# In-place pair differences, earlier residual sums and six landing pages in the second block of a two-block kernel

## The chip, the cores and the metric

One core of a Trainium2 chip runs the whole program. The metric is the device time of one execution in microseconds, the median of several runs. TensorE (PE) does the matrix products, VectorE (DVE), ScalarE (ACT) and GpSimd (POOL) the elementwise work, SyncE (SP) issues nearly all transfers. Each engine works through its own queue in order.

## The reference, cut to what matters

A first block (a gated spatial mixer, then windowed attention) yields x, 1024 tokens by 1024 features. The change lies in the second block:

```
hl = modulate(rmsnorm(x, norm1_g), sh1, sc1)
gate_b, gate_c, hv = split(hl @ conv_w_in, 3)          # 1024 x 3072
yl = (gate_b * conv3_grid(gate_c * hv, conv_w)) @ conv_w_out
x = x + g1 * yl
h = modulate(rmsnorm(x, norm2_g), sh2, sc2)
gate, up = split(h @ ffn_w_in, 2)                      # 2 x 2816 columns
x = x + g2 * ((silu(gate) * up) @ ffn_w_out)
return rmsnorm(x, final_g)
```

All in fp32. The kernel makes an fp32 product from three fp32r products of 512 columns: each operand is split into a high part (a cast on ACT, L106) and a remainder (a subtraction on DVE, L107); high by high, high by remainder and remainder by high are added in PSUM.

## The kernel before, in words

**Seven products.** Every large product of the second block is done in halves of tokens, features and columns with seven half-size products instead of eight (Winograd's form). P1 to P7 need the quarters of the right operand (B11, B21, B12) and four combinations of them (T1 = B22 - B21, T3 = B12 - B22, T2 = B12 - T1, T4 = B11 - T2), and four combinations S1 to S4 of the left one.

**Stages of the second block.** (1) `right_operands` (L1172) forms T1 to T4 of the normalised x per block of 128 tokens and splits them into seven slots (`H`, `HB`), four slices t to a slot. (2) `run_sets` (L1277) runs the sets of 128 output columns of `conv_w_in`, seven products of 12 matmuls each; a set's `use` does the gate and the convolution. After two or three sets a pair of results is complete, and `spill` (L1363) stores B11, B21, B12, forms T1 to T4 on POOL and stores them to DRAM. Beside that `sums` (L1419) forms S1 to S4 of the next weight (`conv_w_out`, `ffn_w_out`): load two blocks into two units, add on POOL, store, load the next, in six steps for each pair; `mix.tick()` takes some of those steps at each set's end. (3) `out_products` (L1428) multiplies by `conv_w_out`: for each of P1, P2, P6, P7, P5, P4, P3 in this order it loads right operand and weight (or weight sum) in pairs of 128 rows, splits them into pages and runs 6 matmuls for each of four token blocks and each index of a pair; P1, P6, P5, P3 add up in PSUM banks 0 to 3, P2, P7, P4 in 4 to 7. Its results go through `out_use` (L1631) and `conv_use` (L1645): gate, residual X2 from DRAM, then `third` (L1610): norm, transposes, modulate, split into slots N3. (4) The same for the feed-forward: four columns in eight-product form (`eight`, its "early" half needs only B11 and B21 of all tokens), 18 sets, `out_products` with `ffn_use` and `fourth` (final norm, output).

**Buffers.** `E` holds 18 units `U(i)` of 128x512. In the sets they are handed out by `Units`, first in first out: `get` takes the oldest free one, so its wait is for whatever still reads it. `RAW` is a ring of landing buffers of 128x1024 (`next_raw`): four in the conv stages, three in the last one. Weights that aren't sums land there, and so do those that `eight` loads. Right operands and sums in `out_products` land in `inner`, a ring of four (conv) or eight (feed-forward). Split pages in `out_products` are a ring too: 8 in the conv stage, 14 in the last.

**Order of the work.** The program order is written by hand, but a planner (with its own estimate of durations) puts each engine's queue in order; it may bring work forward past program order where data and buffers allow. What it can't do is take a ring's buffer before the earlier user in program order has let it go. A transfer, too, holds a buffer until it is done: a store's source can be rewritten only after the store has completed.

Of the kernel before, what the change touches and what calls it, by code (L numbers as in the profile page):

```python
# [10 lines left out]
ALU = mybir.AluOpType  # L11
# [16 lines left out]
def program(tc, I, out):  # L28
# [4 lines left out]
    with ctx:  # L33
# [771 lines left out]
        xs2 = ring([ZX[:, 0:1024]])  # L805
        hs2 = ring([ZX[:, 1024:1536]])
# [7 lines left out]
        junk = sb(P2, "junk", 512)  # L814
# [357 lines left out]
        def right_operands(where, t, h1, h2, eng):  # L1172

            b11, b21, b12, b22 = h1[:, 0:512], h1[:, 512:1024], h2[:, 0:512], h2[:, 512:1024]
            split_slots(("B12",), where, t, b12)
            V.tensor_tensor(b21, b22, b21, ALU.subtract)
            eng.tensor_tensor(b22, b12, b22, ALU.subtract)
            V.tensor_tensor(b12, b12, b21, ALU.subtract)
            eng.tensor_tensor(b11, b11, b12, ALU.subtract)
            split_slots(("T2", "T3"), where, t, h2)  # L1180
            split_slots(("T4", "T1"), where, t, h1)
# [95 lines left out]
        def run_sets(sets, where, units):  # L1277
# [12 lines left out]
            for n, (st, use) in enumerate(sets):  # L1290
# [72 lines left out]
        def spill(dst, j, even, odd, units):  # L1363

            (b11, b12), (b21, b22) = even, odd
            ids = [units.get() for _ in range(4)]
            t1, t2, t3, t4 = (U(i) for i in ids)
            if b11 is None:
                ids += [units.get() for _ in range(2)]
                b11, b21 = (U(i) for i in ids[4:])  # L1370
                SY.dma_start(b11, dst["B11"][j])
                SY.dma_start(b21, dst["B21"][j])
            else:
                SY.dma_start(dst["B11"][j], b11)
                SY.dma_start(dst["B21"][j], b21)
            SY.dma_start(dst["B12"][j], b12)
            G.tensor_tensor(t1, b22, b21, ALU.subtract)
            SY.dma_start(dst["T1"][j], t1)
            G.tensor_tensor(t2, b12, t1, ALU.subtract)
            SY.dma_start(dst["T2"][j], t2)  # L1380
            G.tensor_tensor(t3, b12, b22, ALU.subtract)
            SY.dma_start(dst["T3"][j], t3)
            G.tensor_tensor(t4, b11, t2, ALU.subtract)
            SY.dma_start(dst["T4"][j], t4)
            units.put(*ids)

        def sums_steps(w, j, dst, a, b):

            def block(m, k):
                return w[(2 * j + k - 1) * 128:(2 * j + k) * 128, (m - 1) * 512:m * 512]  # L1390

            def s0():
                SY.dma_start(a, block(2, 2))
                SY.dma_start(b, block(2, 1))

            def s1():
                G.tensor_tensor(a, a, b, ALU.add)
                SY.dma_start(dst["S1"][j], a)
                SY.dma_start(b, block(1, 2))

            def s2():
                G.tensor_tensor(b, a, b, ALU.subtract)
                SY.dma_start(dst["S2"][j], b)
                SY.dma_start(a, block(1, 1))

            def s4():
                G.tensor_tensor(a, a, b, ALU.subtract)
                SY.dma_start(dst["S4"][j], a)
                SY.dma_start(b, block(2, 2))

            def s5():
                SY.dma_start(a, block(1, 2))

            def s3():
                G.tensor_tensor(a, a, b, ALU.subtract)
                SY.dma_start(dst["S3"][j], a)
            return [s0, s1, s2, s4, s5, s3]

        def sums(w, nj, dst, bufs):  # L1419

            steps = []
            for j in range(0, nj, 2):
                two = [sums_steps(w, i, dst, U(bufs[2 * (i - j)]), U(bufs[2 * (i - j) + 1])) for i in range(j, min(j + 2, nj))]
                for x in zip(*two) if len(two) == 2 else [(y,) for y in two[0]]:
                    steps.extend(x)
            return steps
# [109 lines left out]
        for t in range(4):  # L1536
# [7 lines left out]
            right_operands(N1, t, a, b, G if t < 3 else V)  # L1544
# [5 lines left out]
        units = Units(14, 15, 8, 9, 10, 11, 12, 13)  # L1550
        spill(TC, 0, (None, U(16)), (None, U(17)), units)
        units.put(16, 17)
# [20 lines left out]
        def gate(j):  # L1573
            def use(c11, c12, c21, c22, free):
# [4 lines left out]
                spill(TC, j, *((cv[:, 0:512], cv[:, 512:1024]) for cv in cvs), units)  # L1579
                cvs.clear()  # L1580
                if j == 1:
                    mix.begin(sums(c_out, 4, SC, [units.get() for _ in range(4)]), 5)
# [13 lines left out]
        xsr = ring([U(12, 2), U(14, 2)])  # L1596
# [13 lines left out]
        def third(i, xs, junk):  # L1610

            t = i % 4
            SY.dma_start(X3[i], xs)
            for h in range(2):
                mean_square(MS[:, i, h:h + 1], xs[:, h * 512:(h + 1) * 512], junk)
            rms(RM[:, i:i + 1], MS[:, i, :])
            xn, hs = next_raw(), next_raw()
            V.tensor_scalar(xn, xs, RM[:, i:i + 1], None, op0=ALU.mult)
            for h in range(2):
                feature_blocks(xn[:, h * 512:(h + 1) * 512], hs[:, h * 512:(h + 1) * 512], h,  # L1620
# [5 lines left out]
            else:  # L1626
                h1 = next_raw()
                SY.dma_start(h1, HR3[t])
                right_operands(N3, t, h1, hs, G if t < 3 else V)

        def out_use(name, t, ps):  # L1631

            u2, u3, r = U(t), U(4 + t), U(8 + t)
            if name in ("P1", "P6"):
                A.copy(u2, ps)
            elif name == "P2":
                V.tensor_tensor(r, ps, u2, ALU.add)
                G.tensor_tensor(r, r, gbs[0], ALU.mult)
            elif name == "P5":
                A.copy(u3, ps)  # L1640
                V.tensor_tensor(u3, PS[:, 4 + t], u3, ALU.add)
                G.tensor_tensor(u3, u3, gbs[1], ALU.mult)  # L1642
            return u2, u3, r

        def conv_use(name, t, ps):  # L1645
            u2, u3, r = out_use(name, t, ps)
            if name == "P5" and t < 2:
                halves[t]["load"]()
            elif name == "P4":
                xs = xsr()  # L1650
                SY.dma_start(xs, X2[t])
                G.tensor_tensor(xs[:, 0:512], xs[:, 0:512], r, ALU.add)
                V.tensor_tensor(r, ps, u2, ALU.add)
                V.tensor_tensor(r, r, gbs[1], ALU.mult)
                V.tensor_tensor(xs[:, 512:1024], xs[:, 512:1024], r, ALU.add)
                third(t, xs, r)
            elif name == "P3":
                if t == 0:
                    halves[0]["early"](N3, (6, 7), early_up(0))
                xs = xsr()  # L1660
                SY.dma_start(xs, X2[4 + t])
                G.tensor_tensor(xs[:, 512:1024], xs[:, 512:1024], u3, ALU.add)
                V.tensor_tensor(u2, ps, gbs[0], ALU.mult)
                V.tensor_tensor(xs[:, 0:512], xs[:, 0:512], u2, ALU.add)
                third(4 + t, xs, u2)
                if t < 3:
                    f = t + 1
                    if f > 1:
                        halves[f]["load"]()
                    halves[f]["early"](N3, ((0, 6), (1, 7), (2, 0))[t], early_up(f))  # L1670
# [21 lines left out]
        for f in range(4):  # L1692
            halves[f]["late"](N3, ((4, 5), (6, 7))[f % 2], late_up)
            units.put(*halves[f]["keep"])
            if f % 2:
                spill(TF, f // 2, (None, U(ys[0])), (None, U(ys[1])), units)
                units.put(*ys)
                ys.clear()

        def gated_up(f):  # L1700
            def use(c11, c12, c21, c22, free):
# [9 lines left out]
                if f % 2:  # L1711
                    spill(TF, f // 2, *((U(a), U(b)) for a, b in ys), units)
                    units.put(*ys[0], *ys[1])
                    ys.clear()
                if f == 7:
                    mix.begin(sums(f_out, NFF // 2, SF, [units.get() for _ in range(4)]), NFF - 9)
# [13 lines left out]
        xsr = ring([U(12, 2), U(14, 2)])  # L1730

        def fourth(i, halves):
            rms(RX[:, i:i + 1], MS[:, i, :])
            for h in (1, 0):
                c = slice(h * 512, (h + 1) * 512)
                V.scalar_tensor_tensor(halves[h], halves[h], RX[:, i:i + 1], FG[:, c], ALU.mult, ALU.mult)  # L1736
                SQ("l").dma_start(out[0, i * 128:(i + 1) * 128, c], halves[h])

        def ffn_use(name, t, ps):
            u2, u3, r = out_use(name, t, ps)  # L1740
            if name == "P5":
                x = next_raw()[:, 0:512]
                SY.dma_start(x, X3[4 + t][:, 512:1024])
                G.tensor_tensor(u3, u3, x, ALU.add)  # L1744
                mean_square(MS[:, 4 + t, 1:2], u3, x)
            elif name == "P4":
                xs = xsr()
                SY.dma_start(xs, X3[t])
                G.tensor_tensor(xs[:, 0:512], xs[:, 0:512], r, ALU.add)
                V.tensor_tensor(r, ps, u2, ALU.add)  # L1750
                V.tensor_tensor(r, r, gbs[1], ALU.mult)  # L1751
# [60 lines left out]
```

## Time and profile before

| | before |
|---|---|
| median of 3 runs | 2709.69 us (2708.47 to 2711.11) |
| profiled execution, its own time | 2709.77 us |
| its span, first to last instruction | 2708.0 us |
| PE busy | 2588.4 us, 96% |
| DVE busy | 1841.7 us, 68% |
| ACT busy | 1102.5 us, 41% |
| POOL busy | 656.7 us, 24% |
| DMA, mean | 156 GB/s |

The second block starts at about 1623 us of the span. Its sets of the convolution run to about 1890, the product with `conv_w_out` to 1979, the feed-forward's start to 2120, its sets to 2476, the last product to the end. PE is busy nearly all the time, so what a stage loses shows as PE idle or as a lower granted clock after it; a busy share of the whole span doesn't show it, a table of stretches does.

### The profile page before, as it was taken

The page shows a single profiled execution, that of the slowest core. Times are in us where ns is not written, and L with a number is a line of the kernel's source. Part 1 is how long each engine was busy: PE and PEld are TensorE (multiplying, and loading weights), DVE is VectorE, ACT ScalarE, POOL GpSimd, SP SyncE. Part 2 cuts the span into 40 slices and gives each one's busy share as a digit, 9 for nine tenths or more (in the row PEclk, how much of TensorE's full clock was granted, in tenths as well). Part 3 has the DMA queues.
Part 4 walks back from the last instruction along what each step waited for, and adds up shares of the span by engine and source line. Part 5 has one row for each costly group of instructions (what it writes and reads, how often), then busy time and mean ns, then how long its engine had stood idle before and what let it go on. Part 6 is the DMA issues. An engine that isn't in the chain of part 4 may idle for free. (4 is left out here: it accounts for less than half of the span.)

```text
span 2708.0 us, 37147 instructions
## 1 busy us (share of the span) xinstructions
PE 2588.4 (96%) x13666; PEld 2216.0 (82%) x13666; DVE 1841.7 (68%) x3013; ACT 1102.5 (41%) x1979; POOL 656.7 (24%) x634
## 2 busy tenths in 40 slices
PE   8999999999999999999999987999878999999998
PEld 5799998879999778888888876877756877787876
DVE  5677775666778875456677977678566765667536
ACT  4332334322233435345556875223454232334433
POOL 2110000010002412313345762041321345302111
PEclk9999999999999999999999998999989999999999
DMA  7454333364444435541364325356554478538643
GB/s 258 141 148 122 101 119 125 121 205 135 130 137 133 146 103 189 174 155 61 92 244 133 98 78 167 109 183 194 179 181 149 151 253 260 181 103 287 195 151 129
DMA packets 344938, 421.18 MB, mean 156 GB/s; under 512 B 18918, under 2 KB 207870, under 8 KB 344242
## 3 DMA queue, kind: packets, MB, share of 16 engines
q1 hardware_dynamic: 337012, 407.80, 47.0%
q10 hardware_dynamic: 7744, 11.01, 1.1%
q8 instruction: 107, 1.75, 0.3%
q14 instruction: 75, 0.61, 0.1%
HBM read 324.84 MB, written 93.91 MB: 155 GB/s over the span
## 5 line engine op out<-in xcount | busy, mean ns | idle before, releaser
L106 ACT CAST w<-raw 128x1024 fp32r<-128x1024 f32 (+1 forms) x234 | 221.7, 958 | 437.5 <-DMA raw<-in_a_w_in 121.9
L107 DVE TENSOR_TENSOR w<-raw,w 128x1024 fp32r<-128x1024 f32 (+1 forms) x232 | 288.1, 1253 | 152.7 <-ACT w L106 148.3
L1265 PE MATMUL PS<-H,w 128*128 128x512 f32 x1404 | 336.8, 395 | 14.1 <-ACT E L1302 10.7
L1265 PEld LDWEIGHTS PS<-H,w 128*128 128x128 f32 x1404 | 267.2, 191 | 74.5 <-ACT E L1302 12.3
L516 PE MATMUL PS<-H,w 128*128 128x320 f32 x2112 | 320.5, 309 | 1.0 <-DVE TT L525 1.0
L516 PEld LDWEIGHTS PS<-H,w 128*128 128x128 f32 x2112 | 310.8, 188 | 3.1 <-DVE TT L525 1.3
L1456 PE MATMUL PS<-H 128*128 128x512 f32 x924 | 220.4, 397 | 12.3 <-ACT H L106 10.5
L1456 PEld LDWEIGHTS PS<-H 128*128 128x128 f32 x924 | 176.7, 192 | 52.3 <-ACT H L106 12.2
L339 POOL TENSOR_TENSOR H<-ACC,H 128x256 fp32r<-128x256 f32 x52 | 50.3, 968 | 609.6 <-ACT H L338 505.1
L320 DVE SCALAR_TENSOR_TENSOR ACC<-raw,CO,ACC 128x512 f32<-128x512 f32 x182 | 133.8, 747 | 20.6 <-DMA raw<-in_ada_w 17.9
L516 PE MATMUL PS<-H 128*128 128x320 f32 x960 | 144.7, 309 | 0.0
L516 PEld LDWEIGHTS PS<-H 128*128 128x128 f32 x960 | 141.1, 188 | 0.5
L603 PE MATMUL PS<-w,H 128*128 128x512 f32 x600 | 140.1, 391 | 0.0
L1265 PE MATMUL PS<-HB,w 128*128 128x512 f32 x540 | 135.7, 400 | 2.9 <-ACT E L1302 2.5
L603 PEld LDWEIGHTS PS<-w,H 128*128 128x128 f32 x600 | 111.5, 188 | 23.3
L107 DVE TENSOR_TENSOR PTR<-PS,PTR 128x512 fp32r<-128x512 f32 x176 | 106.1, 613 | 35.9 <-ACT PTR L106 34.4
L1265 PEld LDWEIGHTS PS<-HB,w 128*128 128x128 f32 x540 | 102.3, 190 | 28.2 <-ACT E L1302 3.4
L1339 PE MATMUL PS<-H,w 128*128 128x512 f32 x408 | 106.2, 413 | 19.3 <-ACT E L1347 9.1
L392 PE MATMUL PS<-H 128*128 128x512 f32 x510 | 120.9, 391 | 0.0
L870 ACT ACTIVATE s<-s,sm 128x641 f32<-128x641 f32 (+1 forms) x128 | 103.3, 808 | 42.6 <-DVE sm L868 42.0
L107 DVE TENSOR_TENSOR H<-raw,H 128x1024 fp32r<-128x1024 f32 x68 | 88.6, 1306 | 46.6 <-ACT H L106 45.2
L106 ACT CAST H<-raw 128x1024 fp32r<-128x1024 f32 x68 | 70.6, 1043 | 110.1 <-DMA raw<-in_a_w_in 63.2
(356 smaller groups left out, 5201.8 us busy)
## 6 DMA issues: line engine op xcount, KB each, us to landing
raw<-in_a_w_in SPq DMA_DIRECT2D x96, 512.0 KB
raw<-in_ada_w SPq DMA_DIRECT2D x80, 512.0 KB
raw<-in_ffn_w_in SPq DMA_DIRECT2D x76, 256.0 KB
E<-in_ffn_w_out SPq DMA_DIRECT2D x66, 256.0 KB
raw<-in_a_w_out SPq DMA_DIRECT2D x32, 512.0 KB
TFT<-E SPq DMA_DIRECT2D x44, 256.0 KB
SFS<-E SPq DMA_DIRECT2D x44, 256.0 KB
raw<-in_b_w_in SPq DMA_DIRECT2D x20, 512.0 KB
```

The costliest lines, as they stand in the source:

```text
L106: A.copy(hi, src)
L107: turn["split"] = (eng or V).tensor_tensor(lo, src, hif, ALU.subtract)
L320: V.scalar_tensor_tensor(ACC[:, s, :], r[:, j, :], CO[:, c, k:k + 1], ACC[:, s, :], ALU.mult, ALU.add)
L339: G.tensor_tensor(AL.r[:, 256:512], ACC[:, s, c], AL.f[:, 0:256], ALU.subtract)
L392: T.matmul(ps, HT[0][:, k, ap, t * 128:(t + 1) * 128], w[:, k % 2, :], start=k == 0 and n == 0, stop=k == 7 and n == 2)
L516: T.matmul(pss[h][:, 0:320], w[:, k, :], HT[0][:, k, ap, h * 320:(h + 1) * 320], start=k == 0 and n == 0, stop=k == 7 and n == 2)
L603: turn["mm"] = T.matmul(accs[t], ys[j].r[:, ap * 640 + t * 128:ap * 640 + (t + 1) * 128], wv[:, j, :], start=kp == 0 and j == 0 and n == 0 ...
L870: A.activation(out=p[:, :nk + 1], in_=p[:, :nk + 1], func=AF.Exp, scale=-1.0, bias=sm[:, j:j + 1], accum_out=sm[:, 2 + j:3 + j])
L1265: turn["mm"] = T.matmul(ps, w[:, k, :], b[:, ap, k, :], start=start and k == 0 and n == 0, stop=k == 3 and n == 2, skip_group_check=not start)
L1339: turn["mm"] = T.matmul(ps, x[:, k, :], b[:, ap, k, :], start=start and k == 0 and n == 0, stop=stop and k == 3 and n == 2, skip_group_che ...
L1456: turn["mm"] = T.matmul(ps[:, t], x[ap][:, i, t * 128:(t + 1) * 128], s[v][:, i, :], start=new and j + i == 0 and q == 0, stop=j + i == nj ...
```

## The change

- `right_operands`: all four subtractions on DVE (before: two of the four on POOL for t < 3).
- `spill`: T1 to T4 overwrite B21, B22, B12, B11 in place, in the order T1, T3, T2, T4; no units are taken for them. `late_spill` does so for pairs whose B11 and B21 come back from DRAM.
- `sums`: a step now does both indices of a pair of pairs, and `run_sets` has a second `mix.tick()` in the middle of each set; the number of ticks over which the steps are spread goes from 5 to 12 and from 13 to 26.
- `out_use` takes over the residual for both stages: halves of X are loaded where P2, P7, P5 and P4 end, added and squared there, so that P4 and P3 add one half each. P2 and P5 take a landing buffer of `RAW` for each of four token blocks. Every token block has its own units; the ring `xsr` of two goes.
- `third` and `fourth` take the two halves; X3 is stored and normalised in halves.
- `out_products` for `conv_w_out`: 6 landing pages and 7 split pages instead of 4 and 8.
- The small buffer `junk` of the attention is allocated earlier in its pool.

```
-        def right_operands(where, t, h1, h2, eng):
+        def right_operands(where, t, h1, h2):
...
-            eng.tensor_tensor(b22, b12, b22, ALU.subtract)
+            V.tensor_tensor(b22, b12, b22, ALU.subtract)
...
                     head(nxt)
+                mix.tick()
...
+        def spill(dst, j, even, odd):
+            (b11, b12), (b21, b22) = even, odd
+            for name, x in (("B11", b11), ("B21", b21), ("B12", b12)):
+                SY.dma_start(dst[name][j], x)
+            pair_sums(dst, j, b11, b12, b21, b22)
+
+        def pair_sums(dst, j, b11, b12, b21, b22):
+            for name, o, x, y in (("T1", b21, b22, b21), ("T3", b22, b12, b22), ("T2", b12, b12, b21),
+                                  ("T4", b11, b11, b12)):
+                G.tensor_tensor(o, x, y, ALU.subtract)
+                SY.dma_start(dst[name][j], o)
...
+        def out_use(X, name, t, ps, done):
+            u2, u3, r, x = U(t), U(4 + t), U(8 + t), U(12 + t)
+
+            def gated_add(u, gb, i, h):
+                G.tensor_tensor(u, u, gb, ALU.mult)
+                y = next_raw()[:, 0:512]
+                SY.dma_start(y, X[i][:, h * 512:(h + 1) * 512])
+                G.tensor_tensor(u, u, y, ALU.add)
+                mean_square(MS[:, i, h:h + 1], u, y)
+
+            if name in ("P1", "P6"):
+                A.copy(u2, ps)
+            elif name == "P2":
+                V.tensor_tensor(r, ps, u2, ALU.add)
+                gated_add(r, gbs[0], t, 0)
+            elif name == "P7":
+                SY.dma_start(x, X[t][:, 512:1024])
+            elif name == "P5":
+                A.copy(u3, ps)
+                V.tensor_tensor(u3, PS[:, 4 + t], u3, ALU.add)
+                gated_add(u3, gbs[1], 4 + t, 1)
+            elif name == "P4":
+                V.tensor_tensor(u2, ps, u2, ALU.add)
+                V.tensor_tensor(u2, u2, gbs[1], ALU.mult)
+                V.tensor_tensor(u2, u2, x, ALU.add)
+                SY.dma_start(x, X[4 + t][:, 0:512])
+                mean_square(MS[:, t, 1:2], u2, PS[:, 4 + t])
+                done(t, r, u2)
+            else:
+                tmp = next_raw()[:, 0:512]
+                V.tensor_tensor(tmp, ps, gbs[0], ALU.mult)
+                V.tensor_tensor(x, x, tmp, ALU.add)
+                mean_square(MS[:, 4 + t, 0:1], x, tmp)
+                done(4 + t, x, u3)
...
         def conv_use(name, t, ps):
+            if name == "P3" and t == 0:
+                halves[0]["early"](N3, (6, 7), early_up(0))
+            out_use(X2, name, t, ps, third)
             if name == "P5" and t < 2:
                 halves[t]["load"]()
...
-        out_products(c_out, 4, TC, SC, pages[2:], [p.f[:, q * 1024:(q + 1) * 1024] for p in pages[:2] for q in range(2)],
+        out_products(c_out, 4, TC, SC, pages[3:], [p.f[:, q * 1024:(q + 1) * 1024] for p in pages[:3] for q in range(2)],
```

## Rows read from the trace of the kernel before

**Rows 1.** The profiled page: its span, and the group of weight-splitting subtractions.
```profile
span 2708.0 us, 37147 instructions
...
L107 DVE TENSOR_TENSOR w<-raw,w 128x1024 fp32r<-128x1024 f32 (+1 forms) x232 | 288.1, 1253 | 152.7 <-ACT w L106 148.3
```
**Rows 2.** Stretches: length, busy us (count) of PE, PEld, DVE, ACT, POOL, PEclk, DMA, GB/s.
```profile
1620.00:1680.00 60.00, 46.39 (x186) 36.96 (x185) 44.06 (x72) 31.77 (x58) 16.74 (x11) 0.87 0.57 180
...
1880.00:1940.00 60.00, 50.90 (x206) 40.25 (x205) 36.98 (x34) 24.92 (x29) 17.31 (x10) 0.91 0.73 232
1956.00:2000.00 44.00, 29.86 (x134) 23.00 (x132) 31.76 (x63) 21.67 (x51) 14.83 (x13) 0.82 0.46 162
2000.00:2080.00 80.00, 71.70 (x301) 54.90 (x302) 49.69 (x75) 40.33 (x71) 13.85 (x10) 0.97 0.44 141
...
2200.00:2320.00 120.00, 108.85 (x442) 86.67 (x441) 73.47 (x83) 32.19 (x52) 62.39 (x43) 0.94 0.78 256
2320.00:2460.00 140.00, 140.00 (x611) 114.35 (x610) 95.05 (x115) 47.98 (x74) 28.21 (x19) 1.00 0.42 137
...
2620.00:2640.00 20.00, 14.68 (x52) 10.97 (x51) 7.48 (x8) 8.46 (x16) 11.94 (x8) 0.83 0.56 167
2694.00:2708.00 14.00, 0.62 (x3) 0.19 (x1) 9.21 (x20) 2.00 (x6) 2.61 (x4) 0.63 0.55 206
```
**Rows 3.** Waits of PE from 1600 us on: us in total, times, longest.
```profile
PE PS L1265 <- ACT E L1302: 13.2, 6, 4.9
...
PE PS L1339 <- ACT w L106: 7.7, 4, 4.5
```
**Rows 4.** Timeline in the feed-forward's sets, 2196 to 2222 us: start, duration, instruction, idle before.
```profile
2209.92 0.38 SPq L1384 DMA_DIRECT2D TFT<-E  x1
...
2214.56 0.63 ACT L1706 ACTIVATE E<-E 128x512 f32<-128x512 f32 x1 [13.69 <-DMA TFT<-E]
...
2215.72 6.45 PE L1265 MATMUL PS<-H,w 128*128 128x512 f32 x20 [2.41 <-ACT E L1302]
```
**Rows 5.** Waits of SP's queue, 2140 to 2460 us.
```profile
SPq L1382 <- POOL E L1381: 30.9, 6, 10.6
```
**Rows 6.** Timeline at the second block's start.
```profile
1658.51 0.68 DVE L1178 TENSOR_TENSOR E<-E 128x512 f32<-128x512 f32 x1
...
1659.27 4.05 POOL L1179 TENSOR_TENSOR E<-E 128x512 f32<-128x512 f32 x1 [4.21 <-DVE E L1178]
...
1663.35 1.14 ACT L1167 CAST HB<-E 128x512 fp32r<-128x512 f32 x2 [2.69 <-POOL E L1179]
...
1666.44 10.49 PE L1339 MATMUL PS<-H,w 128*128 128x512 f32 x38 [4.50 <-ACT w L106]
```
**Rows 7.** Timeline early in the product with `conv_w_out`.
```profile
1916.11 0.37 SPq L121 DMA_DIRECT2D H<-SCS  x1
...
1919.19 1.04 ACT L106 CAST H<-H 128x1024 fp32r<-128x1024 f32 x1 [2.94 <-DMA H<-SCS]
...
1920.29 13.97 PE L1456 MATMUL PS<-H 128*128 128x512 f32 x48 [6.32 <-ACT H L106]
```
**Rows 8.** Timeline at that product's end: gate multiplications, a store and the wait for it.
```profile
1954.57 7.02 POOL L1642 TENSOR_TENSOR E<-E 128x512 f32<-128x512 f32 x4 [29.71 <-DVE E L1641]
...
1985.09 0.79 SPq L1625 DMA_DIRECT2D HR<-raw  x2
...
1989.85 0.41 DVE L1491 TENSOR_SCALAR raw<-PS,C 128x128 f32<-128x128 f32 x1 [0.65 <-DMA HR<-raw]
```
**Rows 9.** Timeline in the last product, from P5 to P4.
```profile
2633.40 0.63 ACT L922 ACTIVATE raw<-E 128x512 f32<-128x512 f32 x1 [0.51 <-POOL E L1744]
...
2634.15 9.69 SPq L121 DMA_DIRECT2D raw<-in_ffn_w_out  x5
...
2638.47 1.04 ACT L106 CAST H<-raw 128x1024 fp32r<-128x1024 f32 x1 [1.88 <-DMA raw<-in_ffn_w_out]
```
**Rows 10.** Timeline of the tail: the last evacuation of P3.
```profile
2699.19 0.68 DVE L1758 TENSOR_TENSOR E<-PS,E 128x512 f32<-128x512 f32 x1
```

More of the change, by code (lines that the diff above doesn't have):

```diff
@@ L1387, in sums_steps @@
[L1387 to L1417, printed above, removed]
@@ L1421, in sums @@
             steps = []
             for j in range(0, nj, 2):
-                two = [sums_steps(w, i, dst, U(bufs[2 * (i - j)]), U(bufs[2 * (i - j) + 1])) for i in range(j, min(j + 2, nj))]
-                for x in zip(*two) if len(two) == 2 else [(y,) for y in two[0]]:
-                    steps.extend(x)
+                two = [pair(j + i, U(bufs[2 * i]), U(bufs[2 * i + 1])) for i in range(min(2, nj - j))]
+                steps.extend(lambda x=x: [y() for y in x] for x in zip(*two))
             return steps
@@ L1549, in program @@
             halves[n]["late"](N1, (2 * n, 2 * n + 1), late_uses[n])
-        units = Units(14, 15, 8, 9, 10, 11, 12, 13)
-        spill(TC, 0, (None, U(16)), (None, U(17)), units)
-        units.put(16, 17)
+        late_spill(TC, 0, U(16), U(17), U(14), U(15))
+        units = Units(8, 9, 10, 11, 12, 13, 14, 15, 16, 17)
         c_sets = []
@@ L1578, in use @@
                 free()
-                spill(TC, j, *((cv[:, 0:512], cv[:, 512:1024]) for cv in cvs), units)
+                spill(TC, j, *((cv[:, 0:512], cv[:, 512:1024]) for cv in cvs))
                 cvs.clear()
                 if j == 1:
-                    mix.begin(sums(c_out, 4, SC, [units.get() for _ in range(4)]), 5)
+                    mix.begin(sums(c_out, 4, SC, [units.get() for _ in range(4)]), 12)
                 mix.tick()
@@ L1628, in third @@
                 SY.dma_start(h1, HR3[t])
[L1629 to L1643, printed above, removed]
+                right_operands(N3, t, h1, hs)
@@ L1695, in program @@
             if f % 2:
-                spill(TF, f // 2, (None, U(ys[0])), (None, U(ys[1])), units)
-                units.put(*ys)
+                b11, b21 = units.get(), units.get()
+                late_spill(TF, f // 2, U(ys[0]), U(ys[1]), U(b11), U(b21))
+                units.put(*ys, b11, b21)
                 ys.clear()
@@ L1711, in use @@
                 if f % 2:
-                    spill(TF, f // 2, *((U(a), U(b)) for a, b in ys), units)
+                    spill(TF, f // 2, *((U(a), U(b)) for a, b in ys))
                     units.put(*ys[0], *ys[1])
@@ L1715, in use @@
                 if f == 7:
-                    mix.begin(sums(f_out, NFF // 2, SF, [units.get() for _ in range(4)]), NFF - 9)
+                    mix.begin(sums(f_out, NFF // 2, SF, [units.get() for _ in range(4)]), 2 * (NFF - 9))
                 mix.tick()
```

124 lines of the change are left out of this document (43 added, 81 removed).

## The prediction

> **What bounds the kernel now.** The table of stretches comes first, as the page's totals can't tell a stage that loses from one that doesn't: undisturbed, PE runs 611 matmuls of 512 columns in 140 us, 0.229 us each, at clock 1.00, and never idles [rows 2]. Against that price each other row shows its loss: 442 matmuls in the 120 us from 2200, worth 101.2, so 18.8 lost; 206 in the 60 us from 1880, worth 47.2, so 12.8 lost; 52 in the 20 us from 2620, worth 11.9, so 8.1 lost. Where short transposes are mixed in I read idle time alone: 13.6 us in the 60 from 1620, 14.1 in the 44 from 1956, 8.3 in the 80 from 2000, and 13.4 after PE's last matmul [rows 2]. Next come PE's waits and the timeline around each, to see who ends the idle time; [rows 3 to 10] are taken from there. So the kernel is PE-bound between stalls, and the change can only give back stalls, or make new ones.
>
> **The sets of the feed-forward (2200 to 2320).** PE waits for the chain copies L1302 of ACT, 13.2 us in six waits [rows 3]. They are not late themselves: ahead of them in ACT's queue stands a tanh L1706 which waits for a store of T4. That was issued at 2209.92 and released the unit at 2214.56, 4.64 us later; PE resumes at 2215.72 [rows 4]. By the order of `get` and `put`, the unit of the odd column's first result was T4 of the pair before. After the change a spill takes no units: this result then takes a unit that a set's chain sum has left, with no store on it, and the first unit that inherits T4 is the odd column's second result, one set (84 matmuls of 0.229, 19 us) later. What could go wrong is in the in-place order: T1 waits for the store of B21, T2 for that of B12, and behind them on POOL stand sums' additions, behind their stores on SP the weights of the next set. SP already waits up to 10.6 us for POOL there [rows 5] without a PE wait of its own in the list, so one wait of 4.64 us per pair is mostly covered by weights loaded a set ahead. Bounds: +18.8 (all gone) to a loss (rival 1). I take +15. The convolution's sets have the same form; of the 13.2 us, 11.2 at most lie in this stretch (120 less 108.85), so 2.0 lie outside it: I take +2 of them, bounds 0 and +2.
>
> First the row on such a store: 4.64 us from issue to release for 256 KB [rows 4]. The Trainium skill, page "DMA: Bandwidth & Descriptors", section "Anatomy of one DMA — SWDGE (gpsimd) path", says that a transfer's fixed part of about 2.0 us is mostly the wait until the last byte is confirmed in the target memory, before which no semaphore moves; this speaks against writing in place. It is written for the GpSimd path, and no run here shows that path; its formula would give 2.6 us for 256 KB (an estimate), and rival 1 below would then cost 36 us instead of 65.
>
> **More and earlier sum steps.** The additions, loads and stores stay the same in number; only their place in program order moves, and the waits that pace them (POOL for a load, SP for POOL) stay. They run beside 20 us sets that PE fills. Cost 0; bounds -2 to +2 from the same kind of wait as in [rows 5], which today reaches PE nowhere.
>
> **`right_operands` on DVE.** Six subtractions at the first place leave POOL. One of them took 4.05 us there, and a cast that needed it held ACT for 2.69 us; PE then sat idle 4.50 us for a weight cast queued behind [rows 6]. On DVE a subtraction is 0.68 [rows 6]; six add 4.1 us to an engine busy 44.1 of the 60 us [rows 2]. The other idle time of the stretch (a wait of the copy after the first early product) isn't touched. Bounds -4.1 to +4.5; I take +3, near the stall that the row shows.
>
> **`conv_w_out`, its start (1880 to 1940).** The 6.32 us stall ends with a cast at 1919.19 that waited for a sum. Two loads of sums bear on it, one issued only at 1916.11, when a landing page came free [rows 7]. Six pages let such loads go earlier, and `eight`'s weights move to after P2, out of the way. Against it: with 7 split pages P6's first sum takes the page that P1's second right operand holds, so PE must wait for at least one cast, 1.04 [rows 9], and T1, T2, T4 leave some us later than before as T1 waits for B21's store; they are wanted 10 us later. Bounds 0 to +12.8; +6.
>
> **`conv_w_out`, its end (1956 to 2000).** Here the change adds a wait that I find by counting `next_raw` in program order through the ring of four: P1 0, 1; P2 2, 3; P2's residuals 0 to 3; then in P5: residual 0, load 1, 2, residual 3, load 0, 1, residual 2, 3; P4's weights 0, 1. Before, P4's first weight followed a load that was finished early. Now it can't be fetched until P5's first token block is gated, added and squared, and then a page of `eight` has gone through the same buffer. From the first gate multiplication at 1954.57: multiplication 1.75 (7.02 over four), addition 1.75, square 0.8 [rows 8, 9], load 4.3, cast 1.04 [rows 9], subtraction 1.25 [rows 1], load 4.3, cast 1.04: 1970.8. P5's products end near 1957. P3 can't fill the gap: its second pair takes the split page that P4's first right operand holds, so 6 matmuls (1.4 us) go ahead at most. PE idles some 12.5 us. P4 then ends near 1970.8 + 48 x 0.229 at clock 0.9, 1983; its first block near 1978.5. From there the new form is quicker: no ring of two X buffers, X at hand. What remains is DVE, about nine 512-wide passes a block at 0.68 (three residual, two normalising, two's worth of modulation quarters, two split subtractions), 6.1 us, four blocks 24.5: 2003, against 2000 before [rows 2], where the wait for X and for stores such as the 4.76 us from 1985.09 to 1989.85 [rows 8] spread the same blocks. So -3, with PE's P3 inside that time. Bounds -12.5 (nothing absorbs the stall) to +10 (planner and ring kinder than I count).
>
> **The feed-forward's start (2000 to 2080).** 8.3 us idle, 7.7 of PE's waits there and nearby are for weight casts [rows 2, 3]: weights loaded late through the same ring. New order: the third column's weights follow the normalised block 5, not the reload of block 4's left half, so they come some 10 us earlier; six more subtractions on DVE cost 4.1 beside PE. Bounds -8 to +8.3; +5.
>
> **The last product.** P5 to P4 keeps its chain (gate, add, square, load, cast: P4's first weight waits for the second token block as before), so the 8.1 us at 2620 stay: 0, bounds -4 to +4 by one load. In the tail PE is through at 2694.6 [rows 2], but the last evacuation of P3 starts at 2699.19 [rows 10]: DVE still has P4 blocks that waited for the ring `xsr`. With that ring gone it starts as soon as its products are there; what comes after stays. Up to +4.6, at least 0; some matmul records are missing near the end, so +3.
>
> **Sum.** 15 + 2 + 0 + 3 + 6 - 3 + 5 + 0 + 3 = 31 us. The profiled execution took 2709.8 us (span 2708.0), the median of the runs is 2709.7, so both serve: 2679 us, with its own range 2665 to 2693.
>
> **Rivals.**
> 1. *Slower: the in-place waits hold POOL, and SP behind it.* 3 conv and 11 feed-forward pairs, each with a wait of 4.64 for B21's store [rows 4], 65 us in all if nothing covers them: 2679 + 65 = 2744. It decides from 31/14 = 2.2 us exposed per pair on; at that the kernel is where it was. For it: SP's queue is in order and already waits for POOL [rows 5]. Against: those waits reach PE only by T4's unit.
> 2. *The ring of four decides the residual stage.* The full 12.5 us of P4's late weight stay exposed: 9.5 more than forecast, and the +5 after it goes too: 2693. For it: the same chain with one load fewer costs 8.1 us in the last product already. Against: DVE's work after P4 was the longer path before.
> 3. *The stall in the sets only moves* (the change doesn't free what it says, as another unit with a store on it, T1's or T2's, takes the place of T4's): without the 15 + 2, 2696.
> 4. *Everything goes as meant*: 18.8 + 2 + 4.5 + 10 and 5 at the start and end of `conv_w_out` + 8.3 + 4.6 = 53, so 2657.
>
> **How the numbers follow.** Forecast 0.58, rival 1 0.08, rival 2 0.14, rival 3 0.12, rival 4 0.08. The range, 2658 to 2702, holds the forecast, rivals 2 and 3 with some us of play, and leaves out rival 1 and about half of rival 4. A change under 0.2%, 5.4 us, can't be told from none with this kernel. Faster: all but rival 1 and the worst ends of 2 and 3, 0.88; rival 1 gives 0.07 slower; 0.05 the same.
>
> **What would show it.** In the changed trace: no wait of L1706's like for a T store and 520 or more matmuls in the 120 us of sums; no POOL line in `right_operands`; the 6.3 us stall of P6 down to 1 or 2; a new PE gap of 10 us or more between P5 and P4 of `conv_w_out`, ended by a weight cast; the last P3 evacuation within 1 us of its products. Wrong would be: PE waits for left-operand weights in the sets (rival 1), a median above 2702, or no gap before P4.

## The result, and the profile after

The change makes the kernel slower. Median 2724.99 us (2722.16 to 2728.41) against 2710.4 us (2708.47 to 2711.45) of the kernel before in the same job: ratio 1.0055, 95% interval [1.0038, 1.0073], 14.6 us more. The forecast was 2679, its range 2658 to 2702. The profiled span went from 2708.0 to 2720.4 us.

The table counts matmuls in equal stretches of the two traces, as the prediction did, and prices the difference at its 0.229 us. Short transposes are counted too, and as the kernels drift apart the stretches hold slightly different work, so a row is good to about 2 us.

| stretch, us | before | after | gain, us | forecast |
|---|---|---|---|---|
| 1600-1680, second block's entry | 251 | 266 | +3.4 | +3 |
| 1680-1860, convolution's sets | 775 | 788 | +3.0 | +2 |
| 1860-1940, start of `conv_w_out` | 296 | 300 | +0.9 | +6 |
| 1940-2000, its end | 205 | 150 | -12.6 | -3 |
| 2000-2100, feed-forward's start | 388 | 311 | -17.6 | +5 |
| 2100-2500, feed-forward's sets | 1650 | 1663 | +3.0 | +15 |
| 2500-2600 | 442 | 442 | 0 | 0 |
| from PE's last matmul to the end | 13.4 us | 8.1 us | +5.3 | +3 |

The sum is -14.6 (the spans differ by 12.4). Two stretches hold the whole loss. These are stretches of the kernel before, with the columns of [rows 2]:

```profile
1860.00:1880.00 20.00, 20.00 (x90) 16.40 (x89) 15.46 (x18) 9.61 (x11) 0.00 (x0) 1.00 0.60 184
...
1940.00:1960.00 20.00, 20.00 (x89) 16.50 (x88) 12.00 (x12) 9.68 (x12) 5.43 (x4) 1.00 0.23 80
1960.00:2000.00 40.00, 25.86 (x116) 19.73 (x115) 28.67 (x60) 19.30 (x48) 10.83 (x11) 0.80 0.51 179
2000.00:2100.00 100.00, 91.70 (x388) 71.19 (x389) 61.73 (x88) 45.84 (x77) 17.10 (x12) 0.98 0.50 155
```

And these of the kernel after:

```profile
1860.00:1880.00 20.00, 15.56 (x65) 12.37 (x65) 11.74 (x14) 5.15 (x7) 0.00 (x0) 0.97 0.73 239
1880.00:1940.00 60.00, 56.75 (x235) 45.52 (x234) 36.02 (x31) 27.77 (x38) 20.03 (x12) 0.95 0.75 250
1940.00:1960.00 20.00, 9.14 (x34) 6.20 (x32) 8.93 (x9) 9.15 (x15) 12.02 (x8) 0.76 0.33 105
1960.00:2000.00 40.00, 26.69 (x116) 21.66 (x117) 22.56 (x52) 13.30 (x31) 3.22 (x6) 0.80 0.31 105
2000.00:2100.00 100.00, 80.95 (x311) 60.51 (x310) 57.59 (x99) 44.76 (x78) 1.65 (x3) 0.86 0.38 116
...
2200.00:2300.00 100.00, 98.82 (x430) 80.12 (x429) 79.81 (x81) 31.68 (x50) 54.04 (x34) 1.00 0.74 244
2300.00:2400.00 100.00, 89.99 (x376) 72.37 (x375) 58.19 (x72) 31.11 (x48) 37.76 (x26) 0.95 0.67 213
```

PE idles 4.4 us in 1860-1880, where the kernel before has 90 matmuls and no idle time; 24.2 us in 1940-2000 (14.1 before) and 19.1 in 2000-2100 (8.3 before), at a granted clock of 0.76 to 0.86, so between the levels of 1.2 and 2.4 GHz. And the sets still lose 11.2 us of idle time, only later: in 2200-2400 instead of [rows 2]'s 2200-2320. The stretch that the forecast priced gains 68 matmuls, 15.6 us, and the next one, which lost nothing before, loses 54, 12.4 us:

```profile
2200.00:2320.00 120.00, 117.51 (x510) 95.12 (x509) 94.47 (x97) 37.95 (x59) 61.66 (x40) 1.00 0.75 245
2320.00:2460.00 140.00, 131.29 (x557) 106.36 (x556) 84.31 (x110) 44.62 (x68) 37.37 (x25) 0.96 0.49 156
```

The 11.27 us gap of `conv_w_out` is the chain that the prediction counted out of `next_raw`; the timeline shows each link (start, duration, instruction, idle before):

```profile
1946.20 3.50 POOL L1608 TENSOR_TENSOR E<-E 128x512 f32<-128x512 f32 x2 [20.78 <-DVE E L1623]
...
1949.65 2.26 POOL L1611 TENSOR_TENSOR E<-E,raw 128x512 f32<-128x512 f32 x1
...
1951.94 0.63 ACT L922 ACTIVATE raw<-E 128x512 f32<-128x512 f32 x1 [3.33 <-POOL E L1611]
...
1952.69 0.37 SPq L1326 DMA_DIRECT2D raw<-in_ffn_w_in  x1
...
1956.70 1.04 ACT L106 CAST w<-raw 128x1024 fp32r<-128x1024 f32 x1 [1.58 <-DMA raw<-in_ffn_w_in]
...
1959.03 0.38 SPq L121 DMA_DIRECT2D raw<-in_conv_w_out  x1
...
1963.07 1.04 ACT L106 CAST H<-raw 128x1024 fp32r<-128x1024 f32 x1 [2.20 <-DMA raw<-in_conv_w_out]
...
1964.17 2.08 PE L1451 MATMUL PS<-H 128*128 128x512 f32 x4 [11.27 <-ACT H L106]
```

Gate multiplication, residual addition, square, then `eight`'s weights into the freed buffer, cast, subtraction (on DVE at 1957.78), then P4's weights, cast, PE: 18.0 us from 1946.20 to 1964.17, where 16.2 were worked out from [rows 8, 9]. One detail was off: these are the weights of P4's second pair; those of the first were requested at 1939.32 and came in time.

Behind it come P4's first result on DVE, P3's products on PE, the transposes of `third`, and at 2005.05 the first early product of the feed-forward, which starts at 1999.95 in the kernel before (last line):

```profile
1973.72 1.28 DVE L1626 TENSOR_TENSOR E<-PS,E 128x512 f32<-128x512 f32 x2
...
1987.03 0.41 DVE L1486 TENSOR_SCALAR raw<-PS,C 128x128 f32<-128x128 f32 x1 [3.38 <-PE PS L1479]
...
2005.05 7.54 PE L1340 MATMUL PS<-H,w 128*128 128x512 f32 x25 [3.45 <-ACT H L1167]
```

```profile
1999.95 9.16 PE L1339 MATMUL PS<-H,w 128*128 128x512 f32 x29 [0.54 <-ACT H L1167]
```

In the sets PE waits for the chain copy L1302 as in [rows 3, 4], but another instruction stands ahead of it in ACT's queue. POOL's sum waits for its load; the pair difference L1374 stands behind the sum; SP's store L1375 waits for that; the weights L1218 are issued behind the store at 2322.88 and cast at 2327.88; the copy follows, then PE:

```profile
2319.26 1.97 POOL L1392 TENSOR_TENSOR E<-E 128x512 f32<-128x512 f32 x1 [0.86 <-DMA E<-in_ffn_w_out]
...
2321.19 1.29 POOL L1374 TENSOR_TENSOR E<-E 128x512 f32<-128x512 f32 x1
...
2322.51 0.32 SPq L1375 DMA_DIRECT2D TFT<-E  x1
2322.88 1.04 SPq L1218 DMA_DIRECT2D raw<-in_ffn_w_in  x2
...
2327.88 0.62 ACT L106 CAST w<-raw 128x512 fp32r<-128x512 f32 x1 [9.51 <-DMA raw<-in_ffn_w_in]
...
2328.40 0.58 ACT L1302 COPY E<-PS 128x512 f32<-128x512 f32 x1
...
2329.03 4.70 PE L1265 MATMUL PS<-HB,w 128*128 128x512 f32 x12 [5.96 <-ACT E L1302]
```

The tail does what was meant: P3's last evacuation comes 0.45 us after the last matmul ends (2712.79 against 2711.49 + 0.85), where [rows 10] had it 4.6 us late.

### The profile page after: what moved, and what is told of

The parts are those of the page before. It is cut to its first block, busy times and chain, and to the rows that moved or that the text cites. A ratio compares the mean times of both kernels' runs of the same rounds, so it can differ in the third digit from the quotient of the medians.

```text
span 2720.4 us, 37174 instructions
## 1 busy us (share of the span) xinstructions
PE 2592.0 (95%) x13666; PEld 2217.7 (82%) x13666; DVE 1838.7 (68%) x3033; ACT 1104.2 (41%) x1979; POOL 636.6 (23%) x622
## 4 chain that ended last, share of the span: by engine, by line
PE 79%; DMA 7%; DVE 5%; ACT 3%; issue 3%; POOL 2%; SPq 0%; DVEq 0%; POOLq 0%; ACTq 0%
PE PS L1265 17%; PE PS L516 16%; PE PS L1451 8%; PE PS L603 7%; PE PS L676 5%; PE PS L392 5%; PE PS L1340 5%; PE PS L1053 3%; PE PS L998 3%; PE PS L861 2%; PE PS L895 2%; PE PS L883 2%; PE PS L497 1%; DMA raw<-in_ffn_w_in 1%; DMA VY<-in_ada_w 1%
## 5 line engine op out<-in xcount | busy, mean ns | idle before, releaser
L107 DVE TENSOR_TENSOR w<-raw,w 128x1024 fp32r<-128x1024 f32 (+1 forms) x232 | 294.5, 1279 | 186.4 <-ACT w L106 185.7
L1451 PE MATMUL PS<-H 128*128 128x512 f32 x852 | 205.1, 400 | 25.5 <-ACT H L106 21.8
L1451 PEld LDWEIGHTS PS<-H 128*128 128x128 f32 x852 | 163.7, 193 | 63.7 <-ACT H L106 24.2
L1374 POOL TENSOR_TENSOR E<-E 128x512 f32<-128x512 f32 x60 | 99.1, 1652 | 363.1 <-DMA TFB<-E 99.9
L1265 PE MATMUL PS<-HB,w 128*128 128x512 f32 x540 | 138.5, 406 | 11.4 <-ACT E L1302 11.2
L516 PEld LDWEIGHTS PS<-H 128*128 128x128 f32 x960 | 141.1, 188 | 0.5
L1392 POOL TENSOR_TENSOR E<-E 128x512 f32<-128x512 f32 x60 | 96.1, 1609 | 148.7 <-DMA E<-in_ffn_w_out 90.7
L107 DVE TENSOR_TENSOR H<-raw,H 128x1024 fp32r<-128x1024 f32 (+1 forms) x69 | 91.3, 1327 | 55.1 <-ACT H L106 51.8
L392 PE MATMUL PS<-H 128*128 128x512 f32 x510 | 120.8, 391 | 0.0
```

The source lines that it names most:

```text
L107: turn["split"] = (eng or V).tensor_tensor(lo, src, hif, ALU.subtract)
L392: T.matmul(ps, HT[0][:, k, ap, t * 128:(t + 1) * 128], w[:, k % 2, :], start=k == 0 and n == 0, stop=k == 7 and n == 2)
L516: T.matmul(pss[h][:, 0:320], w[:, k, :], HT[0][:, k, ap, h * 320:(h + 1) * 320], start=k == 0 and n == 0, stop=k == 7 and n == 2)
L1265: turn["mm"] = T.matmul(ps, w[:, k, :], b[:, ap, k, :], start=start and k == 0 and n == 0, stop=k == 3 and n == 2, skip_group_check=not start)
L1374: G.tensor_tensor(o, x, y, ALU.subtract)
L1392: G.tensor_tensor(x, a, b, op)
```

## The experiments

Theory A: the ring of four buffers RAW. The landings of P2's and P5's residual halves, and P3's scaled product `tmp`, hold buffers through which the weights of P4 and of the feed-forward's start must pass. Rivals: B, the in-place pair differences and the extra ticks; C, the six landing pages. All ratios are against the kernel before. By their intervals a difference between two rows is good to about 5 us.

| kernel | median, us | ratio | 95% interval |
|---|---|---|---|
| e1 old residual stage of `conv_w_out` | 2702.78 | 0.9973 | 0.9961-0.9985 |
| e2 ring freed there | 2698.69 | 0.9964 | 0.9952-0.9976 |
| e3 kernel before + new residual stage there | 2731.14 | 1.0077 | 1.0064-1.0090 |
| e4 old pair buffers, sums and ticks | 2726.53 | 1.0061 | 1.0049-1.0073 |
| e5 e2 + ring freed in `ffn_w_out` | 2692.23 | 0.9930 | 0.9914-0.9945 |
| e6 e2 + sums' and T stores' transfers from POOL's queue | 2686.74 | 0.9908 | 0.9892-0.9923 |
| e7 e2 + four landings | 2690.41 | 0.9928 | 0.9912-0.9944 |
| e8 e2 + old pair buffers | 2697.31 | 0.9950 | 0.9937-0.9964 |
| e9 `tmp` alone off the ring | 2714.56 | 1.0016 | 1.0005-1.0028 |
| e10 kernel before + six landings | 2712.55 | 1.0008 | 0.9998-1.0019 |
| e11 e6 + old pair buffers | 2700.24 | 0.9963 | 0.9951-0.9975 |
| e12 e5, e6 and e7 together | 2669.80 | 0.9854 | 0.9839-0.9868 |

**e1.** `conv_use` and `third` of the kernel before, with `xsr`; the rest as changed.

> The changed kernel with only the residual stage of conv_w_out put back to the old form (whole X2 rows after P4 and P3, ring xsr, no landing in RAW before P4); in-place sums, extra ticks, six landing pages, subtractions on DVE and the new residual of ffn_w_out stay. Theory A (ring of four: the landings of P2's and P5's residual halves hold RAW, so P4's first weights, the reloads and the weights of the feed-forward's start come late): the two traces part by 30 us between 1940 and 2100, so this gives most of that back, 2725 - 25 = 2700 (2692 to 2708), and PE's 11.3 us gap before P4 is under 3. Rival B (in-place pair differences with the extra ticks hold POOL and SP): no change, 2720 to 2728. Rival C (six landing pages leave five split pages, so P3's second pair can't fill in before P4): the gap before P4 stays over 8 us, 2715 to 2725.

2702.8, 22 us back. The gap is gone, so the loss lies in the residual stage, against B and C.

**e2.** The new stage with other buffers:

```diff
-                y = next_raw()[:, 0:512]
-                SY.dma_start(y, X[i][:, h * 512:(h + 1) * 512])
-                G.tensor_tensor(u, u, y, ALU.add)
-                mean_square(MS[:, i, h:h + 1], u, y)
+                G.tensor_tensor(u, u, x, ALU.add)
+                mean_square(MS[:, i, h:h + 1], u, x)
...
-                tmp = next_raw()[:, 0:512]
+                tmp = u2
```

(`x`, U(12 + t), is loaded after P1 with P2's half, after P7 with P5's, after P5 with P4's, after P4 with P3's.)

> The changed kernel with its early residual additions kept, but all their landings taken off RAW: x, which is free at that time, takes X2's half for P2, then for P5, then for P4, then for P3, and P3's product is scaled into u2. Same instructions, same transfers. Theory A: P4's first weights are free of P5's blocks again, gap before P4 under 4 us instead of 11.3, and one landing fewer in each of P3's blocks: 2725 - 15 = 2710 (2700 to 2715). If it is not the ring but DVE and ACT order or the early additions on POOL themselves: 2722 to 2728 with the gap as it was. Rival C: gap stays, 2720 to 2727.

2698.7, better than expected: what cost time was not the early additions but their buffers. That they gain anything over the late ones is not shown, as the intervals of e1 and e2 overlap. Its stretches:

```profile
1860.00:1880.00 20.00, 15.50 (x67) 12.42 (x66) 12.82 (x14) 6.30 (x8) 0.00 (x0) 0.96 0.85 276
...
1940.00:1960.00 20.00, 20.00 (x88) 16.35 (x88) 15.16 (x17) 9.31 (x17) 12.81 (x8) 1.00 0.25 84
...
2000.00:2100.00 100.00, 91.36 (x384) 70.96 (x383) 59.66 (x81) 39.35 (x62) 7.08 (x4) 0.97 0.48 142
```

1940-1960 has no idle time, and the feed-forward's first product comes 12.8 us earlier than in the changed kernel:

```profile
1992.30 1.65 PE L1340 MATMUL PS<-H,w 128*128 128x512 f32 x3 [2.71 <-ACT H L1167]
```

The stall in 1860-1880 is still there.

**e3.** e1 turned round: the kernel before with the new `out_use` and `third` in `conv_w_out`.

> The kernel before with only the residual stage of conv_w_out in the new form. Theory A: slower than before by 20 to 30 us, 2730 to 2740, with a gap of 8 us or more before P4 that the kernel before does not have. Rival B or C: within 5 us of before, 2705 to 2715.

The loss came (21 us), the gap did not: PE waits 0.98 and 2.57 us and then runs P3's products, as four landings leave one more split page. It gains nothing by it:

```profile
1959.49 12.12 PE L1456 MATMUL PS<-H 128*128 128x512 f32 x41 [2.57 <-DVE H L107]
...
2006.06 4.30 PE L1339 MATMUL PS<-H,w 128*128 128x512 f32 x11 [3.45 <-ACT H L1167]
```

The feed-forward's first product starts at 2006.06, later still, and 2000-2100 has 307 matmuls. So the gap was no loss by itself. The ring delays P4's second pair, from it `third`, and that the start of the feed-forward, whether PE stands or runs P3 meanwhile.

**e4.** `spill`, `sums` and the ticks of the kernel before, in the changed one.

> The changed kernel with the pair differences in buffers of their own, the sums' steps and their ticks put back as before; the rest of the change stays. Theory A: the stall in the feed-forward's sets is 11 us in both kernels, so 2721 to 2729, no change. Rival B: 2725 - 15 = 2710 or less. If the in-place order is worth what was forecast (15 us in the sets): 2738 to 2742.

2726.5, the changed kernel's time: B falls, and with it the forecast's +15 as a net gain. PE's waits for L1302 are 15.3 us here, 11.2 in the changed kernel. Two differences balance: the changed kernel has 35 matmuls more in the sets (788 for 770 in 1680-1860, 1663 for 1646 in 2100-2500), 8.0 us, and 27 fewer at the start of `conv_w_out` (300 for 327), 6.2 us.

**e5.** e2's buffers in `ffn_w_out` too.

> The kernel of e2_free_ring (2698.7, ratio 0.9964) with the residual halves of ffn_w_out off the ring as well. Theory A: the last product's gap between P5 and P4 (5.3 to 8 us idle in every kernel so far, 2640 to 2660) is the same chain, landing in RAW, gate, add, square, then P4's weights; without it the gap falls under 2 and the time to 2694 (2690 to 2697). If that gap is the evacuation of P5 or ACT's order instead: 2697 to 2701.

2692.2, and the last product's gap, 5.5 us idle in 2640-2660 of the changed kernel (52 matmuls), is closed. As e5 runs earlier, the stretches before that one have to be seen too (in e2 the gap lies in 2620-2640, with 53 matmuls):

```profile
2600.00:2640.00 40.00, 40.00 (x177) 33.01 (x177) 22.20 (x20) 19.40 (x28) 13.01 (x8) 1.00 0.51 158
2640.00:2660.00 20.00, 20.00 (x90) 16.54 (x89) 14.09 (x24) 7.49 (x13) 0.04 (x1) 1.00 0.10 28
```

**e6.** The sums' loads and stores and the T stores from POOL's queue.

```diff
-                SY.dma_start(dst[name][j], o)
+                G.dma_start(dst[name][j], o)
...
-                    SY.dma_start(dst[name][j], x)
+                    G.dma_start(dst[name][j], x)
...
-                    SY.dma_start(a, block(2, 2))
-                    SY.dma_start(b, block(2, 1))
+                    G.dma_start(a, block(2, 2))
+                    G.dma_start(b, block(2, 1))
...
```

> The kernel of e2_free_ring, with the loads and stores of the weight sums and the stores of the pair differences started from POOL's own queue instead of SP's; nothing else moves. Theory D (in the feed-forward's sets the weights of a coming set are requested late because their requests stand on SP behind stores that wait for POOL; the cast that waits for them holds the chain copy L1302, and that PE): PE's waits for L1302 fall from 10.7 us to under 4, 2698.7 - 8 = 2691 (2686 to 2695). Theory E (the memory traffic itself makes the weights late, 0.75 of the DMA engines' time at 244 GB/s there): no change, 2696 to 2702, or slower by the cost of POOL's issuing.

2686.7, 12.0 us under e2. PE's waits for L1302 are gone, and 2200-2400 has no idle time, at 227 and 221 GB/s of traffic. The changed kernel loses 10.0 us in 2300-2400 at only 213 GB/s, so the traffic by itself was not the cause; the requests' place in SP's queue, as in the chain above, is what the edit took away:

```profile
2200.00:2300.00 100.00, 100.00 (x437) 81.68 (x436) 79.01 (x87) 34.18 (x54) 66.20 (x80) 1.00 0.71 227
2300.00:2400.00 100.00, 100.00 (x437) 81.76 (x436) 75.01 (x82) 33.98 (x52) 71.46 (x84) 1.00 0.70 221
```

**e7.** `pages[2:]` and four landings.

> The kernel of e2_free_ring with two pages (four landings) and the rest as split pages in conv_w_out, as before the change. If six landings bring what was forecast for the start of conv_w_out (6 us): 2698.7 + 6 = 2705. If the start is governed by when the weights of the feed-forward leave ACT and DVE free: 2696 to 2701, and 285 to 300 matmuls in the 80 us from 1860 as with six.

Faster, not slower, and below both ranges: 2690.4, 8.3 us under e2. The start of `conv_w_out` has 325 matmuls, e2's 294:

```profile
1860.00:1880.00 20.00, 19.33 (x85) 15.59 (x84) 17.13 (x20) 7.12 (x9) 0.00 (x0) 1.00 0.74 236
1880.00:1940.00 60.00, 56.09 (x240) 44.32 (x239) 38.34 (x32) 31.50 (x41) 20.78 (x12) 1.00 0.80 267
```

The stall that goes is this one of the changed kernel, where a cast of a landed right operand waits 8.24 us for its load ahead of the chain copy that PE needs:

```profile
1877.29 1.04 ACT L106 CAST H<-H 128x1024 fp32r<-128x1024 f32 x1 [8.24 <-DMA H<-TCB]
1878.24 0.58 ACT L1302 COPY E<-PS 128x512 f32<-128x512 f32 x1
...
1878.39 1.41 PE L1451 MATMUL PS<-H 128*128 128x512 f32 x3 [4.44 <-ACT H L106]
```

**e8.** The old `spill` in e2.

> The kernel of e2_free_ring with the pair differences in buffers of their own again, extra ticks kept. If writing in place pays by itself: 2703 to 2712, with a wait of L1706's like for a store of T4. If the in-place order costs as much as it gives (T1 waits for B21's store, 5.6 us before the last T1 of the convolution): 2694 to 2700.

2697.3, the same as e2 within their intervals: while SP's queue holds the weights back, writing in place is worth nothing on balance. Against e2 there are 22 matmuls fewer in the sets (777 for 788, 1649 for 1660), 5.0 us, and 19 more at the start of `conv_w_out` (313 for 294), 4.4 us. The stall in 1860-1880 is gone here (89 matmuls). With six landings and the in-place order together, 1860-1940 holds 291 to 304 matmuls in every run (the changed kernel, e1, e2, e5, e6, e9); with only one of the two 313 to 331 (e4, e7, e8, e10, e12), except e11 with 298; the kernel before, with neither, has 296. How they meet is not settled.

**e9.** One line of the changed kernel.

```diff
-                tmp = next_raw()[:, 0:512]
+                tmp = next_raw()[:, 0:512] if X is X3 else u2
```

> The changed kernel with one line changed: in conv_w_out P3's scaled product goes to u2 instead of the next buffer of the ring; the residual halves of P2 and P5 still land in RAW. It splits the 26 us that e2_free_ring gave back. If P5's landings do it all (P4's weights late, and everything after with them): 2720 to 2726, gap of 11 us before P4, and 311 matmuls in the 100 us from 2000. If the fourth buffer per token block in P3 does the second part (17 us between 2000 and 2100): 2725 - 15 = 2710 (2705 to 2714), gap unchanged and 370 or more matmuls from 2000 to 2100.

10.4 us back, between the two expectations, with the gap as it was (11.06 us); 2000-2100 goes from 311 to 352 matmuls:

```profile
2000.00:2100.00 100.00, 86.46 (x352) 67.06 (x353) 60.31 (x100) 46.71 (x80) 1.06 (x2) 0.89 0.46 139
```

So of the 26.3 us that e2 returned, 10.4 belong to `tmp`, and the other 15.9, by subtraction, to the residual halves' landings, each good to some 5 us.

**e10.** Six landings in the kernel before.

> The kernel before with only the six landing pages (and so one split page fewer) in conv_w_out. Forecast of the prediction's step: 6 us faster, 2704. By e7_four_landing_pages (four pages 8 us better than six where the ring is free): slower or the same, 2710 to 2718, with PE idle in 1860 to 1880, where the kernel before is never idle, as casts of landed right operands stand ahead of the last sets' chain copies in ACT's queue.

2712.6, no difference that can be told: the second range, without its sign. 1880-1940 gains 21 matmuls (227 for 206), 4.8 us, without idle time in 1860-1880; 1940-2000 gives 12 of them back and 2000-2100 another 10 (378 for 388), and PE's waits for L1302 in the sets are 15.4 us instead of 13.2.

**e11.** e6 with the old pair buffers.

> The kernel of e6_sums_on_pool_queue with the pair differences in buffers of their own again (e8's spill, its T stores on POOL's queue too). If the store of T4 that holds a unit is a stall of its own, hidden so far behind the late weights: it loses the 10 to 15 us that the prediction gave to writing in place, 2697 to 2702, with PE waiting for L1302 behind a tanh that waits for a store. If the unit's wait was itself SP's lateness (the store issued late behind SP's waits): 2685 to 2690, the same as e6.

2700.2: with SP out of the way the in-place form is worth 13.5 us (ratio 0.9963 against 0.9908). The number is close to what the forecast gave to it, the reason only in small part. In the feed-forward's sets two tanhs wait for a T store (4.55 us at 2127, 3.95 at 2415), and PE waits behind neither; in the convolution's sets a chain copy L1302 waits 4.51 us for one, and PE 1.96 behind it. PE's two longest waits in the feed-forward's sets, 2.63 and 2.53 us, stand behind DVE, whose passes lengthen beside POOL:

```profile
2360.23 4.25 DVE L1747 SCALAR_TENSOR_TENSOR E<-E 128x512 f32<-128x512 f32 x1
...
2360.82 1.30 POOL L1396 TENSOR_TENSOR E<-E 128x512 f32<-128x512 f32 x1
...
2362.63 1.30 POOL L1380 TENSOR_TENSOR E<-E 128x512 f32<-128x512 f32 x1
...
2368.52 0.73 PE L1265 MATMUL PS<-H,PA 128*128 128x512 f32 x2 [2.53 <-DVE E L1306]
```

Why the old buffers make more of this than the new ones is open: DVE is busy 264.8 us in 2120-2450 here, 246.5 in e6.

**e12.** e5, e6 and e7 together.

> The changed kernel with its three faults taken out together: residual halves off the ring in both output stages, sums' and pair differences' transfers on POOL's queue, four landing pages in conv_w_out. If they add: 2724.9 - 26.3 (e2) - 6.5 (e5) - 12 (e6) - 8.3 (e7) = 2672 (2666 to 2680). If the start of conv_w_out and the sets share a cause: 2680 to 2686.

2669.8: the three add. It is 55.2 us faster than the changed kernel and 1.46% [1.32%, 1.61%] faster than the one before. The start of `conv_w_out` has 248 matmuls at clock 1.00 (206 before), and 2200-2400 has no idle time:

```profile
2200.00:2300.00 100.00, 100.00 (x437) 81.78 (x436) 84.51 (x87) 35.12 (x53) 67.26 (x81) 1.00 0.68 217
2300.00:2400.00 100.00, 100.00 (x436) 81.73 (x435) 74.81 (x83) 33.75 (x52) 65.58 (x78) 1.00 0.70 224
```

Not all of it mends the change: the sums' requests stood on SP in the kernel before too, and no run moved them there alone.

## Why the prediction was wrong

**The feed-forward's start** (+5 forecast, -17.6 measured, outside its own bounds of -8 to +8.3): the costliest step. It looked at when the weights are requested after block 5, and took the ring as lightened. But P3's new `tmp = next_raw()` is a fourth buffer per token block beside `xn`, `hs` and `h1`; the count of `next_raw` stopped at P4's weights and never reached it. The first `tmp` is written at 1995.14 in the changed kernel and at 1985.90 in e9, which gives 10.4 us back; with the landings off the ring too (e2) the stretch has 384 matmuls, 388 before. The gain did not come either: with the ring free PE still idles 8.6 us there, 8.3 before. Its price was misread: of the 7.7 us of waits for weight casts [rows 3] 4.5 are the one stall of [rows 6], priced in the entry already, and only 3.2 lie in 1995-2100 (6.4 in the changed kernel).

**The end of `conv_w_out`** (-3 forecast, -12.6 measured): up to P4's weights the chain was right link by link. What failed is what follows, "So -3, with PE's P3 inside that time". From P4's first block to the end of `third` it gave DVE 24.5 us (1978.5 to 2003); the trace takes 31.3, from 1973.72 to the first early product at 2005.05. Part of that is DVE's wait of 3.38 us for `third`'s first transposes, which stand on PE behind P3's products. Also, the chain was worked out in the times of the kernel before, while the sum booked the gains ahead of it (7.3 us by 1940 in the table): the chain starts 8.4 us earlier than in [rows 8], and the feed-forward's first product comes 5.1 us later, so the stage loses that head start too. e3 shows the loss with PE's gap nearly filled, e2 shows it gone. Rival 2 named the mechanism at 2693, 14 us over the forecast; with `tmp` it is 26.3 (e2).

**The sets of the feed-forward** (+15 forecast, +3.0 measured): the cover was wrong. "SP already waits up to 10.6 us for POOL there [rows 5] without a PE wait of its own in the list, so one wait of 4.64 us per pair is mostly covered by weights loaded a set ahead" took SP's wait as harmless because another wait showed up last. The wait that the change aimed at did go: between 1680 and 2480 us it was 55.5 us in the kernel before, and 1.4 are left in the one after. The line of the kernel before (us, times, longest):

```profile
ACT E L1706 <- DMA TFT<-E: 55.5, 5, 16.2
```

The weights on SP were the next wait right behind T4's unit, so taking the unit's wait out moved the stall (rival 3 in effect, though no unit was its cause). e6 removes this second wait, and e2's 10.7 us for L1302 all go.

**The start of `conv_w_out`** (+6 forecast, +0.9 measured): the 6.32 us stall of [rows 7] did go, and 1880-1940 gained 29 matmuls, 6.6 us; but a new stall ahead of it, in 1860-1880, took 5.7 back (65 matmuls for 90). Six landings alone gain there (e10, 317 for 296), and so does the in-place order with four landings (e7, 325); the forecast added up steps that do not add. Why is open.

**Right:** the entry (+3.4, and POOL has left `right_operands`), the convolution's sets (+3.0), the last product (its gap 5.5 us, 5.3 before; e5 confirms that it was the same chain), the tail (+5.3, a little over its bound of +4.6). Rival 1 did not come. Four waits of POOL, 99.9 us in all, end with a store of a pair's quarters, but three of them last over 30 us, far longer than the 4.64 us of a store [rows 4], so most of it is time without work; the fourth is 0.80. PE pays for none of it that the trace shows, and e8 finds the two forms equal on balance.

The prediction also said that no run shows a transfer started by GpSimd; e6, e11 and e12 do (see the last section).

The table's gains without the two rows that the ring spoilt sum to 15.6 us; e2, the changed kernel with that ring freed, is 11 us faster than the one before (2710.0 in the same job, interval [0.9952, 0.9976]).

## What to carry to other kernels

When a change puts new landings into a shared ring of buffers, count every take in program order to the end of the stage, and ask which request stands next in the same buffer: the price is not the engine's gap at that point but how late the next stage's first operand comes (e3). A wait that reaches the bound engine nowhere today can be the next one in line; before a stall is booked as a gain, look in the same queue for what ends second (e6). And an early operation is best given a buffer that was idle anyway: the same additions cost 26 us with RAW that they don't cost with `x` (e2).

## What the runs showed of the hardware

Started from POOL's queue, a T store of 256 KB occupies POOL for 0.56 us (e6, median of 44), against 0.34 for the same store's issue on SP (changed kernel). Such transfers land after these median times (size, then us from issue to landing, in e6's view of DMA issues):

```profile
E<-in_ffn_w_out POOLq DMA_DIRECT2D x66, 256.0 KB, 4.1
...
TFT<-E POOLq DMA_DIRECT2D x44, 256.0 KB, 3.5
...
TCT<-E POOLq DMA_DIRECT2D x16, 256.0 KB, 2.7
```

The formula of the Trainium skill, "DMA: Bandwidth & Descriptors", section "Anatomy of one DMA — SWDGE (gpsimd) path", which gave 2.6 us (an estimate) in the prediction, lies under these 2.7 to 4.1 us, taken beside other transfers; the measurement decides.

A DVE pass of 0.68 us took 4.25 in e11 while POOL ran two subtractions and its issues one after another. The same line with one input in PSUM never takes longer than 0.69 us in that run (durations in ns: shortest, median, longest):

```profile
L1747 DVE SCALAR_TENSOR_TENSOR E<-E x20: 678/692/4252, 2111.9 to 2450.4; 128x512 f32<-128x512 f32 x20
L1747 DVE SCALAR_TENSOR_TENSOR E<-E,PS x16: 674/680/690, 2170.8 to 2469.0; 128x512 f32<-128x512 f32 x16
```

The Trainium skill, "SBUF — State Buffer", section "SBUF: two separate sides", says that a DVE instruction with two SBUF inputs and a GpSimd instruction that reads SBUF block each other for the whole instruction, whichever starts first going first. The rows agree with a wait of that kind between two SBUF inputs and POOL; the order they do not bear out, as the DVE record starts 0.59 us before the first subtraction's (2360.23 against 2360.82) and ends behind the second. No run here took one of the two away to prove it.
